# Thirteen low parts from GpSimd to VectorE, and small reorderings, in a one-core decoder step

## The chip, the core and the metric

The kernel runs on one NeuronCore of a Trainium2 chip. Its engines each work through their own instructions in program order: TensorE (PE, with PEld for its weight loads), VectorE (DVE), ScalarE (ACT), GpSimd (POOL) and SyncE (SP), which here issues the DMAs. They meet through semaphores. The metric is the device time of one launch in microseconds (us), as the median of several runs; beside it there is one profiled execution, from which all trace rows come.

## The reference

One layer of a decoder with three parallel branches is computed in float32 for 1024 prompt positions and 32 sample positions (8 sequences of 4), 1056 columns together, with a model width of 1024.

```python
h = _rmsnorm(x, norm_g)
p = h @ w_in                    # ret q, k, v, g | sgu u, v | xattn q | three gates
o_ret = retention(q, k, v, g)   # 4 heads, rotary, chunks of 128, group norm, silu gate
o_sg = _sgu_branch(gelu(su), gelu(sv), sg_ln_g, sg_ws, sg_bs)    # spatial gating unit
o_x = _xattn(xq, mk, mv)        # 4 heads into 256 memory tokens
merged = g_ret * (o_ret @ w_br_ret) + g_sg * (o_sg @ w_br_sg) + g_x * (o_x @ w_br_x)
x = x + merged @ w_o
z = _rmsnorm(x, norm_ffn_g) @ w_up
zc = conv_b + sum(conv_w[j] * zp[:, j:j + L] for j in range(3))  # causal, width 3
a, b = split(zc)
x = x + (gelu(a) * b) @ w_down
y = _rmsnorm(x, norm_final_g)
```

## The kernel before

**Three products for one.** Activations lie with the model dimension on the 128 partitions and the 1056 positions along the free dimension. Every float32 product is made as three products of a reduced type: each operand is split into a high part (a cast, on ACT) and a low part (operand minus high part, a `tensor_tensor` subtraction on DVE or POOL), and PE adds high x high, high x low and low x high in PSUM.

**Weight slabs.** The weights come as slabs of 128 x 1024 in the order of `SLABS`. `w_prep` loads a slab two ahead, casts it on ACT (line 152) and subtracts on POOL (`ptt`, line 117) or, for the slabs listed in `LO_DVE`, on DVE (`vtt`, line 114). At most three slabs are alive in most stages; `w_ahead` prepares the next one at fixed places of a product, usually right after its first eighth (k = 0) and its fourth (k = 3). In the trace a slab's parts are called `wh` and `wl`.

**The order of the work** is written out by hand. Each engine runs its instructions strictly in the order in which the program issues them. `hook()` is called after each eighth of a product (`fm`) or after each row tile (`tm`): it counts down the entries of `later(n, fn)`, which run n hooks on, takes one entry of the `side` list, and adds `rate[0]` to a counter; each time this reaches one, the next step of the first generator in `gens` is issued. So the small work of the neighbouring stage is laid between the large products. Entries of `later` leave their list in order only.

**The stages**, with the names that the change touches:

- *Heads 0 to 3*: q, k, g and v products, with retention of the head before beside them. In head 0, `fm2` interleaves q and k while the input is loaded. `xnorm` beside it sums the squares of x (tile `xr`, DVE additions), splits the sum (`rsh`, `rsl`), multiplies it by ones on PE and forms the reciprocal root `rst`. `rope_evac` evicts q and k: a product with cos on DVE, swapped halves copied by ACT, a product with sin on POOL, and an addition on DVE by `later(4, ...)`.
- *Gating unit*: products su and sv; `ln_row` normalizes rows; `sgu()` multiplies four groups of 128 rows per step (`sgW`), adds a bias (`sgt`, from PSUM) and multiplies into `su`, both on DVE. The products xq 1 to 3 run at the same time, and slabs xq 2 and xq 3 are prepared in the first half of xq 1.
- *Cross-attention*: the generator `xattn(h)` for each head, beside the gate products gb 0 to 7. Its steps are listed in one table (XA scores, XB transposes, XC values, Y for the samples; `KS`, `VS` and `QS` split keys, values and queries). `gate(key)` makes a gate product, evicts it on DVE (`th`) and returns `gate_out`: a tanh on ACT, and three hooks later a store.
- *Output product*: 8 tiles (m) for each of two halves of 528 columns, with one slab per tile and half, `("wo", m, half)`, and two PSUM banks in turn. After each tile DVE adds it to `x2c`, ACT squares, DVE adds to `ssq`. During the second half the generator `half_norm` works on the first: the sums are split (`ns`), PE multiplies them by ones, DVE scales each `x2c` and makes its low part `xl`; two steps per tile. `early1` adds sums of weights for the next stage (`fs`).
- *Up product, convolution, gate*: pairs of slabs by a seven-product scheme, taps of the convolution on DVE (`c`).
- *Down product*: 22 slabs in groups of two (`down(g)`), eight tiles each; DVE adds every tile to `x2t` (`x` in the trace). `last_conv`, the last pair's five convolution steps, runs as a generator beside group 0, one step per hook with `rate[0] = 1.0`.
- *Final norm*: the last two groups run chunk by chunk over the columns (512, 288, 256). `fin_evac` adds tiles, squares (`sq`, ACT) and sums (`ssf`, DVE). `fin(c)` for the first two chunks is a generator: it splits the sums (`sy3`, `sy` in the trace), forms the root `rsy` and multiplies out eight `y` on POOL. For the last chunk the sum over m = 0 to 5 is split into `sy3`, and the squares of m = 6 and 7 go into PE's sum directly (`fin_last`).

## Time and profile before

| | |
|---|---|
| median of 3 runs | 1917.12 us (1916.00 to 1917.32) |
| profiled execution, own time | 1916.06 us |
| its span, first to last instruction | 1913.9 us |
| mean granted TensorE clock | 0.991 |
| busy: PE, DVE, POOL, ACT | 97%, 60%, 48%, 34% |
| data moved by DMA | 204.82 MB, 107 GB/s on average |

A row of the timeline gives start, duration, engine, line, operation, output <- inputs by the program's names, shape and count of merged instructions, and in brackets the engine's idle time just before and who ended it. A row of the waits gives the waiting engine, tile and line, who released it, the total, the number of times and the longest. A row of the stretches gives the length, then busy time and instruction count of PE, PEld, DVE, ACT and POOL, the granted clock, the DMA share and GB/s. PE's busy time comes from modelled ends of pipelined products, so its idle gaps are somewhat rough. A line number is often that of a helper, so tiles tell more.

### The profile page before, as it was taken

What the parts mean: (1) busy time and instruction counts of PE and PEld (TensorE: products, weight loads), DVE (VectorE), ACT (ScalarE), POOL (GpSimd) and SP (SyncE); (2) the same over time, 40 slices, a digit from 0 to 9 for tenths busy, and PEclk for the clock granted to TensorE, in tenths of its full rate; (3) what the DMA queues carried; (4) which work ended last, traced back from release to release, by engine and by line L of the source; (5) the groups of instructions that cost most, each with busy time, mean ns of one, the idle gap of its engine ahead of it and who ended that gap; (6) DMA issues with size and microseconds to landing.
All of it is one profiled execution on the core that took longest, in us unless ns stands there. A gap on an engine that the chain in (4) does not pass through costs nothing.

```text
span 1913.9 us, 32100 instructions
## 1 busy us (share of the span) xinstructions
PE 1854.7 (97%) x13369; PEld 1828.0 (96%) x13369; DVE 1144.7 (60%) x1610; ACT 651.8 (34%) x1016; POOL 921.5 (48%) x583
## 2 busy tenths in 40 slices
PE   8899999999999999999999999899999999999997
PEld 8899999999999998999999999899999999999996
DVE  6554545442464479332352267999999999744447
ACT  6333232421233434323211233544344344321204
POOL 2243434221643421555544533577777777754404
PEclk9999999999999999999999999999999999999998
DMA  5112131324133341426632532022222223732202
GB/s 189 54 45 93 44 105 36 132 66 156 56 135 112 124 181 55 135 90 255 241 124 79 189 140 84 34 90 79 68 90 79 67 90 120 252 133 90 76 1 91
DMA packets 59808, 204.82 MB, mean 107 GB/s; under 512 B 6608, under 2 KB 9840, under 8 KB 59664
## 3 DMA queue, kind: packets, MB, share of 16 engines
q1 hardware_dynamic: 59664, 202.78, 30.8%
q8 instruction: 105, 1.72, 0.4%
q14 instruction: 39, 0.32, 0.1%
HBM read 154.34 MB, written 48.41 MB: 106 GB/s over the span
## 4 chain that ended last, share of the span: by engine, by line
PE 50%; DVE 7%; issue 1%; ACT 1%; POOL 1%; DMA 1%; DVEq 0%; SPq 0%; POOLq 0%; ACTq 0%
PE bp L108 25%; PE mp L108 25%; DVE c L120 1%; DVE xl L114 1%; DVE x2c L120 1%; DVE fs L114 1%; DVE ssf L114 0%; DMA opr<-scr 0%; POOL opl L117 0%; DMA wr<-in_wslab 0%; DVE x L114 0%; ACT xh L1153 0%; DVE hx L114 0%; POOL acl L117 0%; POOL wls L117 0%
## 5 line engine op out<-in xcount | busy, mean ns | idle before, releaser
L117 POOL TENSOR_TENSOR wl<-wr,wh 128x1024 fp32r<-128x1024 f32 x107 | 282.7, 2645 | 438.3 <-ACT wh L152 294.7
L108 PE MATMUL bp<-xh,wh 128*128 128x264 f32 (+1 forms) x1376 | 279.2, 284 | 6.8 <-DVE th L114 2.4
L108 PE MATMUL bp<-xh,wl 128*128 128x264 f32 (+1 forms) x1376 | 280.3, 285 | 1.2 <-POOL wl L117 0.7
L108 PE MATMUL bp<-xl,wh 128*128 128x264 f32 (+1 forms) x1376 | 279.8, 285 | 0.0
L108 PEld LDWEIGHTS bp<-xh,wh 128*128 128x128 f32 x1376 | 215.0, 189 | 8.2 <-issue 3.1
L108 PEld LDWEIGHTS bp<-xh,wl 128*128 128x128 f32 x1376 | 215.0, 189 | 1.8 <-POOL wl L117 1.2
L108 PEld LDWEIGHTS bp<-xl,wh 128*128 128x128 f32 x1376 | 214.5, 189 | 0.0
L108 PE MATMUL mp<-hh,wh 128*128 128x384 f32 (+1 forms) x816 | 190.0, 340 | 4.9 <-ACT hh L111 4.8
L108 PE MATMUL mp<-hl,wh 128*128 128x384 f32 (+1 forms) x816 | 179.6, 327 | 0.3 <-DVE hl L120 0.3
L114 DVE TENSOR_TENSOR x<-x,mp 128x288 f32<-128x288 f32 (+3 forms) x167 | 105.7, 676 | 120.6 <-PE mp L108 120.6
L108 PE MATMUL mp<-hh,wl 128*128 128x384 f32 (+1 forms) x816 | 177.6, 324 | 0.0
L117 POOL TENSOR_TENSOR wl<-fs,wh 128x1024 fp32r<-128x1024 f32 x52 | 146.2, 2814 | 50.9 <-ACT wh L1179 50.4
L108 PEld LDWEIGHTS mp<-hh,wh 128*128 128x128 f32 x816 | 136.0, 191 | 7.8 <-ACT hh L111 5.4
L108 PEld LDWEIGHTS mp<-hl,wh 128*128 128x128 f32 x816 | 136.6, 190 | 1.1 <-DVE hl L120 1.0
L108 PEld LDWEIGHTS mp<-hh,wl 128*128 128x128 f32 x816 | 137.0, 189 | 0.0
L108 PE MATMUL mp<-ach,whs 128*128 128x384 f32 (+3 forms) x524 | 124.3, 326 | 4.0 <-DVE x L114 3.1
L120 DVE SCALAR_TENSOR_TENSOR c<-z,hist,c 128x1024 f32<-128x1024 f32 x88 | 125.0, 1420 | 4.3 <-ACT c L111 4.2
L108 PE MATMUL mp<-ach,wls 128*128 128x384 f32 (+3 forms) x524 | 123.7, 325 | 0.0
L108 PE MATMUL mp<-acl,whs 128*128 128x384 f32 (+3 forms) x524 | 123.4, 325 | 0.0
L152 ACT CAST wh<-wr 128x1024 fp32r<-128x1024 f32 x86 | 89.4, 1043 | 95.8 <-PE mp L108 54.2
L1179 ACT CAST wh<-fs 128x1024 fp32r<-128x1024 f32 x55 | 57.7, 1050 | 155.6 <-DVE fs L114 145.3
L120 DVE SCALAR_TENSOR_TENSOR c<-zs,hist,c 128x32 f32<-128x32 f32 x88 | 110.6, 1256 | 0.0
(367 smaller groups left out, 4161.5 us busy)
## 6 DMA issues: line engine op xcount, KB each, us to landing
wr<-in_wslab SPq DMA_DIRECT2D x162, 512.0 KB, 3.7
sg<-th SPq DMA_DIRECT2D x24, 528.0 KB, 5.2
th<-sg SPq DMA_DIRECT2D x24, 528.0 KB, 5.5
sca<-c SPq DMA_DIRECT2D x22, 528.0 KB, 3.0
opr<-sca SPq DMA_DIRECT2D x22, 528.0 KB, 4.7
opr<-scr SPq DMA_DIRECT2D x16, 528.0 KB, 7.0
scr<-ort SPq DMA_DIRECT2D x8, 528.0 KB, 7.6
hx<-in_xT SPq DMA_DIRECT2D x8, 528.0 KB, 5.9
```

The lines of the kernel that those rows point to most:

```text
L108: nc.tensor.matmul(out=out, lhsT=l, rhs=r, start=start, stop=stop)
L114: nc.vector.tensor_tensor(out=out, in0=a, in1=b, op=op)
L117: nc.gpsimd.tensor_tensor(out=out, in0=a, in1=b, op=op)
L120: nc.vector.scalar_tensor_tensor(out=out, in0=a, scalar=s, in1=b, op0=op0, op1=op1)
L152: nc.scalar.copy(out=hi, in_=raw)
L1179: nc.scalar.copy(out=hi, in_=src)
```

## The change

- `LO_DVE` grows: the low parts of the eight slabs of the output product's second half, of xq 2 and 3, and of the first head's g 0, g 1 and (v, 0, 0) are subtracted on DVE.
- The rotary addition of the first head runs 7 hooks after its eviction, not 4.
- In the table of `xattn`, the next head's query split `QS` moves ahead of its second key split `KS`.
- The tanh of the gb gates, with the store behind it, runs two hooks after the product.
- `last_conv` advances by one step per two hooks.
- In `fin`, the first chunk's first four `y` are multiplied on DVE; the second chunk's norm starts two steps later.
- The last chunk's sum has a tile of its own, `sy4`, and holds m = 0 to 2 only; the five squares of m = 3 to 7 go into PE's sum directly.

```diff
 LO_DVE = [k for i, k in enumerate(SLABS) if k[0] in ("km", "vm") and i % 2] + [("sv", 0, 0), ("sv", 0, 1)]
+LO_DVE += [("wo", m, 1) for m in range(8)]
+LO_DVE += [("xq", 2), ("xq", 3), ("g", 0), ("g", 1), ("v", 0, 0)]
...
-            later(4, lambda: vtt(out, out, sw, ALU.add))
+            later(4 if h else 7, lambda: vtt(out, out, sw, ALU.add))
...
                            (XC, 1), (XB, 2), (XA, 3), (YC, 0), (XC, 2), (KS, h + 1, 0), (XB, 3), (YC, 1),
-                           (KS, h + 1, 1), (XC, 3), (QS, h + 1), (YD,)):
+                           (QS, h + 1), (KS, h + 1, 1), (XC, 3), (YD,)):
...
-            gate(("gb", m))()
+            later(2, gate(("gb", m)))
...
         gens.append(last_conv())
-        rate[0] = 1.0
+        rate[0] = 0.5
...
-        sy3 = slot("sy3", F32R)
+        sy3, sy4 = slot("sy3", F32R), slot("sy4", F32R)
...
-            yield
+            for _ in range(3 if c else 1):
+                yield
...
-                    ptt(y[:, i, 0:w], x2t[m + i][:, c0:c0 + w], r, ALU.mult)
+                    (vtt if c == 0 and m < 4 else ptt)(y[:, i, 0:w], x2t[m + i][:, c0:c0 + w], r, ALU.mult)
...
-            mm(a, ones, sy3[:, 0:w], stop=False)
-            mm(a, ones, sy3[:, w:2 * w], start=False, stop=False)
-            for i in range(2):
-                mm(a, f(ones), sqs[i], start=False, stop=(i == 1))
+            mm(a, ones, sy4[:, 0:w], stop=False)
+            mm(a, ones, sy4[:, w:2 * w], start=False, stop=False)
+            for i in range(len(sqs)):
+                mm(a, f(ones), sqs[i], start=False, stop=(i == len(sqs) - 1))
...
-                if c == 2 and m > 5:
+                if c == 2 and m > 2:
                     last_sq.append(sqs[m])
...
-            if c == 2 and us[-1] == 5:
-                nc.scalar.copy(out=sy3[:, 0:w], in_=ssf[:, sl])
-                vtt(sy3[:, w:2 * w], ssf[:, sl], f(sy3[:, 0:w]), ALU.subtract)
+            if c == 2 and us[-1] == 2:
+                nc.scalar.copy(out=sy4[:, 0:w], in_=ssf[:, sl])
+                vtt(sy4[:, w:2 * w], ssf[:, sl], f(sy4[:, 0:w]), ALU.subtract)
```

## The prediction

> **What bounds the kernel now.** I read the head of the page first.

> ```profile
> span 1913.9 us, 32100 instructions
> PE 1854.7 (97%) x13369; PEld 1828.0 (96%) x13369; DVE 1144.7 (60%) x1610; ACT 651.8 (34%) x1016; POOL 921.5 (48%) x583
> ```

> TensorE (PE) sets the time, and the change takes no product away from it. What can be won is PE's idle time, 1913.9 - 1854.7 = 59 us, and any time that PE works at a lower clock. So I read next who kept PE waiting (us in total, times, longest).

> ```profile
> PE ap L108 <- ACT rsh L337: 5.9, 1, 5.9
> ...
> PE mp L108 <- DVE x L114: 3.1, 2, 2.6
> PE ap L108 <- DVE sgt L114: 3.0, 1, 3.0
> PE mp L108 <- DVE x2c L120: 2.7, 2, 2.0
> ...
> PE ap L108 <- DVE xql L114: 2.1, 1, 2.1
> PE ap L108 <- ACT sy L319: 1.9, 1, 1.9
> PE ap L108 <- DVE ns L114: 1.7, 1, 1.7
> PE ap L108 <- DVE pt L114: 1.6, 3, 0.9
> ...
> PE ap L108 <- ACT xt L111: 1.3, 1, 1.3
> ```

> These nine rows hold 23 us, nearly all behind VectorE (DVE). Each lies in a stage that the change touches: rsh in the first head, sgt in the gating unit, xql, pt and xt in cross-attention, ns and x2c in the output product's second half, x in the down product, sy in the final norm. Then the stretches in which the granted clock (the figure ahead of the DMA share) is about a half:

> ```profile
> 48.70:52.10 3.40, 0.69 (x1) 0.29 (x1) 3.40 (x3) 2.19 (x3) 0.12 (x1) 0.52 0.14 54
> 52.10:55.50 3.40, 3.19 (x11) 3.19 (x12) 0.71 (x2) 1.69 (x2) 3.40 (x9) 0.50 0.06 4
> ...
> 530.00:533.40 3.40, 2.98 (x12) 2.98 (x13) 3.18 (x6) 0.00 (x0) 0.00 (x0) 0.52 0.84 274
> 1154.60:1158.10 3.50, 3.50 (x19) 3.50 (x18) 3.50 (x3) 1.34 (x2) 2.64 (x1) 0.53 0.19 73
> ...
> 1656.40:1659.80 3.40, 2.83 (x10) 2.86 (x11) 3.40 (x5) 1.45 (x2) 3.40 (x2) 0.52 0.20 38
> 1891.90:1895.30 3.40, 3.08 (x14) 3.08 (x15) 3.15 (x7) 1.47 (x4) 2.64 (x2) 0.52 0.41 154
> ```

> Each follows one of the stalls of 1.9 us or more, lasts 3.4 us, and costs a busy PE half of that, 1.7 us. A long stall is thus paid nearly twice. The stall of 2.1 us (xql) has no such stretch, so about 2 us is where it becomes a matter of position.

> **What makes DVE late.** Rows of DVE and GpSimd (POOL) in order of time:

> ```profile
> 43.78 2.38 POOL L117 TENSOR_TENSOR wl<-wr,wh 128x1024 fp32r<-128x1024 f32 x1
> ```

> ```profile
> 44.34 5.52 DVE L114 TENSOR_TENSOR xr<-xr 128x1056 f32<-128x1056 f32 x3 [4.19 <-ACT xr L111]
> 49.77 1.25 DVE L114 TENSOR_TENSOR k<-k,sw 128x1056 f32<-128x1056 f32 x1
> ```

> ```profile
> 728.33 1.23 DVE L114 TENSOR_TENSOR wl<-fs,wh 128x1024 fp32r<-128x1024 f32 x1 [1.17 <-ACT wh L1179]
> ```

> Three additions cost 5.52 us where one of their size costs 1.25: 5.52 - 3.75 = 1.77 us too much, just the time until POOL's subtraction ends (43.78 + 2.38 - 44.34 = 1.82). While POOL subtracts, a DVE instruction with two SBUF operands stands. So a low part moved from POOL to DVE takes a block of up to 2.4 us away and adds 1.23 us of DVE's own.

> **The change part by part**, against the profiled run (1916.06 us with the 2.2 us around its span).

> *First head.* Slab (v,0,0) is the 43.78 row. On DVE its low part falls into the 4.19 us in which DVE waits for ScalarE (ACT), so 1.77 us come back. The two g slabs held earlier additions in the same way, and K's eviction behind them; I count 0.8 more for that, nothing to 1.8 as bounds. The later addition (7 hooks for 4) changes only which of two equal ones (1.25) stands between the sums and the low part rsl: Q's now, K's before. Sum **-2.6**, from -1.0 to -4.3 (one of the two half-clock stretches may go).

> *Gating unit.*

> ```profile
> 523.79 5.98 DVE L114 TENSOR_TENSOR su<-su,sgt 128x512 f32<-128x512 f32 x1
> ```

> ```profile
> 523.30 1.27 POOL L117 TENSOR_TENSOR sgS<-sgS,sgW 32x512 f32<-32x512 f32 x1 [0.71 <-DVE sgS L886]
> 524.54 4.67 POOL L117 TENSOR_TENSOR wl<-wr,wh 128x1024 fp32r<-128x1024 f32 x2
> ```

> One product takes 5.98 us because POOL runs three instructions in a row; the last two are xq 2 and 3, the moved ones. After the change DVE does 2 x 1.23 us ahead of its first sgt, and PE, whose third group needs that one's bank, waits for it: 1.2 us, or 2.4 if sgS (1.27) comes between. The stall of 3.0 becomes 1.2 to 2.4, and the half-clock stretch goes surely at 1.2 and by half a chance at 2.4. **-2.4**, from -0.5 to -3.5.

> *Queries split sooner.*

> ```profile
> 590.79 2.55 DVE L114 TENSOR_TENSOR xql<-xq,xqh 128x1056 fp32r<-128x1056 f32 x1 [3.15 <-ACT xqh L293]
> ```

> The split comes one step earlier, ahead of the key split: it no longer lies behind a slab's cast on ACT nor under that slab's subtraction. The eviction of the gate product queues behind it on DVE for some 1.3 us; its bank is wanted only a whole product later, which covers that (uncovered it would cost these 1.3). The stall of 2.1 goes. **-2.1**, from -1 to -2.1.

> *Tanh later.*

> ```profile
> 643.43 1.18 ACT L111 ACTIVATE th<-th,vecs 128x1056 f32<-128x1056 f32 x1 [0.63 <-DVE xrc L976]
> ```

> ```profile
> 699.07 2.47 DVE L120 SCALAR_TENSOR_TENSOR hx<-hx,vecs,rst 128x1056 f32<-128x1056 f32 x1
> ```

> Behind each tanh on ACT stand the slab's cast, and through it POOL's subtraction, and the cast of pt: 1.18 us sooner for both. That covers the 0.9 of pt; and a subtraction that ends earlier no longer doubles hx, on which xt (1.3) waits. The tanh itself lands two hooks on, perhaps ahead of another softmax; its store moves with it and is read long after. **-1.5**, from -2.9 to +1.

> *Output product, second half.*

> ```profile
> 1087.15 1.05 ACT L152 CAST wh<-wr 128x1024 fp32r<-128x1024 f32 x1 [1.48 <-DMA wr<-in_wslab]
> ```

> ```profile
> 1122.27 2.45 DVE L114 TENSOR_TENSOR ns<-ssq,ns 128x528 fp32r<-128x528 f32 x1 [0.76 <-ACT ns L1476]
> ...
> 1146.37 0.71 DVE L114 TENSOR_TENSOR ssq<-ssq,sq 128x528 f32<-128x528 f32 x1 [0.71 <-ACT sq L111]
> 1146.99 0.69 DVE L114 TENSOR_TENSOR fs<-fr 128x512 f32<-128x512 f32 x1
> 1147.60 2.88 DVE L114 TENSOR_TENSOR fs<-fr,fs 128x512 f32<-128x512 f32 x1
> 1150.40 0.76 DVE L120 SCALAR_TENSOR_TENSOR x2c<-x2c,vecs,rst 128x528 f32<-128x528 f32 x1
> 1151.08 0.70 DVE L114 TENSOR_TENSOR xl<-x2c,xh 128x528 fp32r<-128x528 f32 x1
> ...
> 1167.30 0.71 DVE L120 SCALAR_TENSOR_TENSOR x2c<-mp,x2c 128x528 f32<-128x528 f32 x1 [1.96 <-PE mp L108]
> ...
> 1173.12 0.71 DVE L120 SCALAR_TENSOR_TENSOR x2c<-mp,x2c 128x528 f32<-128x528 f32 x1 [2.59 <-PE mp L108]
> ```

> PE gives a tile each 1173.12 - 1167.30 = 5.82 us. DVE's turn for one, unblocked: eviction 0.71, wait for the square 0.71, sum 0.71, two scalings and two low parts 2 x (0.76 + 0.70) = 2.92; that is 5.05, and with a moved low part 6.3, more where it waits for ACT's cast (1.05, queued behind the square): some 6.7. Two turns add 2 x 0.69 for fs. So for four tiles DVE is slower than PE, with one tile's grace, since there are two banks. Before, POOL added blocks like 2.88 - 0.69 = 2.2 to each turn. Walking through the turns I get 0.6 at the norm (the first low part, 1.23, stands ahead of ns, in place of a block of 2.45 - 0.71 = 1.7), then 1.1 and 1.7 at the banks: 3.4 against 1.7 + 2.7 = 4.4. The longest is below 1.9, so the stretch at 1154.60 goes too (1.7). **-2.7**, from -6.1 (all of it) to +3 (each long turn 1 us longer than I have it). The first two of the eight low parts are made in the first half, where DVE has no scalings and low parts (the 2.92) to do and waits for PE; they cost nothing there, and 1.23 each if DVE were full.

> *Last convolution at half the rate.*

> ```profile
> 1653.17 2.42 DVE L120 SCALAR_TENSOR_TENSOR c<-zs,hist,c 128x32 f32<-128x32 f32 x1
> ```

> A 32-column tap takes 2.42 us under POOL's subtractions, and with one tap after each of five tiles the evictions (x) fall behind: 3.1 us of stall and the stretch at 1656.40, 4.8 in all. With one tap after every second tile DVE has two tiles' time for it. I keep 0.9 for one blocked tap. **-3.9**, from -1.9 to -4.8.

> *Norms at the end.*

> ```profile
> 1883.26 11.28 POOL L117 TENSOR_TENSOR y<-x,rsy 128x512 f32<-128x512 f32 x8 [68.59 <-DVE rsy L120]
> ```

> ```profile
> 1884.10 3.71 DVE L114 TENSOR_TENSOR ssf<-ssf,sq 128x288 f32<-128x288 f32 x3
> ```

> ```profile
> 1903.55 1.13 PE L108 MATMUL ap<-sq,ones 128*128 128x256 f32 x4 [0.44 <-ACT sq L111]
> ```

> POOL's eight y stretch DVE's sums; the sums make sy late (1.9) and bring the stretch at 1891.90 (1.7). Four y go to DVE, two of them ahead of the evictions on which PE's next chunk waits: +0.7 to +2. The second norm starts two hooks on, so sy is ready, but its y's run later and can lie beside the last norm on POOL and DVE: +0 to +2. Three more squares go into the closing sum, which per square costs 1.13 / 2 = 0.57, some 1.7, in place of ACT's and DVE's chain of about the same length. I take **0**, from -3.6 to +2.5.

> **The sum** is -2.6 - 2.4 - 2.1 - 1.5 - 2.7 - 3.9 = -15.2: 1916.06 to 1900.9, and as the median of the runs shown (1917.12) lies 1.06 higher, **1902 us**.

> [...]

> **Rivals.** (1) *DVE inherits.* It takes POOL's place as the late one: the product's turns are 7.5 instead of 6.7, so that its stalls and stretch stay (0), the gating unit gives 0.6, the tail costs 2.5, tanh gives 1.0, the convolution 2.2; with 2.6 and 2.1 that is -6.0: **1911**. For it: turns longer than 5.82. Against: 2.2 us blocks go. (2) *The half-clock stretches stay* wherever they fall, and only stalls shrink: without the clock's share (1.2 in the gating unit, 1.7 each in the product, the convolution and the tail) the sum is -8.9: **1908**. For it: the stall of 2.1 without a stretch. Against: six stretches, each behind a stall. (3) *Slower: the evictions stand behind the slabs.* On POOL nobody stands behind a low part that waits for a cast; on DVE the evictions do. If slabs m2 to m7 come late by the 1.48 us of the row above, a turn is 6.7 + 1.5 = 8.2: six tiles cost 2.4 each, 14.3, and a stretch behind each, 10.2; less the 6.1 of before that is +18.4, against -12.5 elsewhere: **1923**. It decides from about 1.2 us of lateness (then +16.3). Against: in the second half no cast waits so long. (4) *The wait only changes sides*: DVE's own 1.23 and POOL's shifted work eat what the blocks gave, and 2 us remain: **1915**. [...]

> **How the numbers follow.** Forecast 0.55, (1) 0.22, (2) 0.09, (4) 0.08, (3) 0.06. Below 0.2% (3.8 us) this kernel's runs tell no change. Faster is the forecast, (1) and (2): 0.86; same is (4): 0.08; slower is (3): 0.06. All lower bounds together would give 1890; the range goes three quarters of the way there from the forecast, to 1893, and up to 1912, which takes in rivals 1 and 2; the forecast's own is 1896 to 1908.

> **What would show it.** No POOL subtraction beside the additions before rsh, and rsh near 48.3; su without a 6 us row; no xql among PE's waits; DVE turns near 6.7 in the output product, with stalls of 1 to 1.7 and no half clock there; no half clock in the down product. I am wrong if PE waits longer for x2c than 2.7 in total, if the tail after the last product grows by over 2 us, or if stretches at half clock number as many as before.

## The result and the profile after

The changed kernel takes **1900.57 us** (median; 1900.39 to 1901.69), the kernel before 1916.56 us beside it: ratio 0.9918, 95% interval 0.9901 to 0.9935. That is 16.0 us faster, the interval lies well below 1, and it is 1.4 us below the forecast of 1902. The profiled execution went from 1916.06 to 1901.69 us; of the four runs of the changed kernel it is the slowest, by 1.1 us. The sum came out; several of its terms did not.

The head of the page after the change, and the waits of PE in that trace (total, times, longest):

```profile
span 1899.8 us, 32104 instructions
PE 1851.4 (97%) x13375; PEld 1827.2 (96%) x13375; DVE 1141.8 (60%) x1624; ACT 652.1 (34%) x1016; POOL 888.0 (47%) x566
```

```profile
PE mp L110 <- DVE x L116: 6.8, 5, 2.0
...
PE ap L110 <- ACT rsh L339: 3.1, 1, 3.1
...
PE mp L110 <- DVE x2c L122: 1.2, 2, 0.9
...
PE ap L110 <- DVE sgt L116: 0.9, 1, 0.9
...
PE ap L110 <- DVE ns L116: 0.6, 1, 0.6
...
PE ap L110 <- ACT sy L321: 0.2, 1, 0.2
```

Of the nine rows shown for before, xql, pt and xt are gone; sgt fell from 3.0 to 0.9, rsh from 5.9 to 3.1, x2c from 2.7 to 1.2, ns from 1.7 to 0.6, sy from 1.9 to 0.2. One grew: x, from 3.1 to 6.8 (two waits of 2 us in the down product, two new ones of 1.6 and 0.7 in the tail). The stretches at half clock that are left before the closing chain, in the same columns as before:

```profile
47.92:51.33 3.41, 1.87 (x5) 1.47 (x6) 3.41 (x3) 3.38 (x4) 1.50 (x1) 0.50 0.00 0
51.33:54.75 3.42, 3.42 (x13) 3.42 (x12) 2.58 (x2) 0.90 (x2) 3.42 (x11) 0.50 0.37 107
...
1211.87:1215.28 3.41, 3.23 (x14) 3.23 (x15) 3.38 (x5) 2.23 (x5) 1.97 (x3) 0.50 0.47 144
```

There are two more, at 225.4 (as before) and at 1652.2 in the down product. Gone are those of the gating unit, the output product and the tail.

**Where the time went.** PE's instructions are the same in both traces, in the same order up to number 13301. So the start of instruction k after, less its start before, is all that was won up to there, whatever the waits are called:

| PE instruction | start before | start after | shift | in this stage |
|---|---|---|---|---|
| 224, ahead of rsh | 44.84 | 45.50 | +0.66 | start and load +0.66 |
| 1400, head 1 | 220.84 | 219.28 | -1.56 | first head -2.2 |
| 3500 | 517.25 | 515.92 | -1.33 | +0.2 |
| 3590 | 534.67 | 529.86 | -4.80 | gating unit -3.5 |
| 4010 | 596.72 | 589.45 | -7.27 | queries' split -2.5 |
| 4760 | 706.69 | 693.75 | -12.94 | cross-attention, pt and xt -5.7 |
| 7650 | 1117.59 | 1104.29 | -13.30 | -0.4 |
| 7960 | 1161.88 | 1144.54 | -17.34 | output product -4.0 |
| 11700 | 1625.83 | 1609.68 | -16.15 | up product +1.2 |
| 13200 | 1876.09 | 1862.17 | -13.92 | down product +2.2 |
| end of span | 1913.94 | 1899.83 | -14.11 | tail -0.2 |

The +0.66 at the start is within what the load varies between executions: over the kernels below it lies between -0.6 and +0.9. Each kernel has one trace, so a stage's shift holds for one execution.

### The profile page after: what moved, and what is told of

Its sections match the earlier page's. It is cut to its first block, busy times and chain, and to the rows that moved or that the text cites. A ratio compares the mean times of both kernels' runs of the same rounds, so it can differ in the third digit from the quotient of the medians.

```text
span 1899.8 us, 32104 instructions
## 1 busy us (share of the span) xinstructions
PE 1851.4 (97%) x13375; PEld 1827.2 (96%) x13375; DVE 1141.8 (60%) x1624; ACT 652.1 (34%) x1016; POOL 888.0 (47%) x566
## 4 chain that ended last, share of the span: by engine, by line
PE 52%; DVE 7%; issue 1%; ACT 1%; DVEq 0%; POOL 0%; ACTq 0%
PE bp L110 27%; PE mp L110 25%; DVE c L122 2%; DVE xl L116 1%; DVE x2c L122 1%; DVE x L116 0%; DVE fs L116 0%; DVE wl L116 0%; DVE hx L116 0%; DVE z L116 0%; ACT xh L1155 0%; DVE ssf L116 0%; DVE c L116 0%; ACT sq L113 0%; DVE y L116 0%
## 5 line engine op out<-in xcount | busy, mean ns | idle before, releaser
L119 POOL TENSOR_TENSOR wl<-wr,wh 128x1024 fp32r<-128x1024 f32 x94 | 250.5, 2669 | 374.2 <-ACT wh L154 223.2
L122 DVE SCALAR_TENSOR_TENSOR c<-z,hist,c 128x1024 f32<-128x1024 f32 x88 | 129.9, 1477 | 4.6 <-ACT c L113 4.5
```

The lines of the kernel that those rows point to most:

```text
L119: nc.gpsimd.tensor_tensor(out=out, in0=a, in1=b, op=op)
L122: nc.vector.scalar_tensor_tensor(out=out, in0=a, scalar=s, in1=b, op0=op0, op1=op1)
```

## The experiments

All kernels start from the changed one; each was timed beside the kernel before (medians 1916.45 to 1916.69 us), and its ratio is to that. Medians alone don't settle parts of 1 to 3 us here (the runs of one kernel lie up to 6 us apart; more at the end), so each part is read from PE's positions too.

**The last convolution at full rate again.**

```diff
-        rate[0] = 0.5
+        rate[0] = 1.0
```

> The changed kernel with the last convolution at its full rate again (one step after each tile, as before). In the changed kernel's trace PE waits 1.96 and 2.04 us for x in the down product and has a half-clock stretch at 1652.2; the same products of PE lie 2.1 us later than the shift ahead of the stage would put them. Theory A (the steps were only moved to where POOL subtracts without a pause; at the full rate two of the four taps come before the first subtraction, 1.5 us each in place of up to 5.8): the stage gives 2 us back, about 1898.5 us. Rival B (the stalls come from the phase in which slabs reach POOL, whatever the rate): within 0.5 us of the changed kernel, 1900 to 1901. Rival C (the forecast's reading, half the rate wins): 1903 or more.

1899.85 us, ratio 0.9912 (0.9897 to 0.9926). From instruction 11700 to 13200 PE loses 0.3 us against before, where the changed kernel loses 2.2. PE waits 0.5 and 2.6 us for x and has one stretch. The median gained only 0.7. Rival C, the forecast's reading, is out, for it asked for 1903 or more. Theory A would have it that half the rate costs the 1.9 between the two traces, and that is not shown: the six kernels below that keep half the rate lie between -0.7 and +0.7 us against before in this stage, so much of the changed kernel's 2.2 goes with the moment at which POOL's slabs arrive, as rival B has it (in its trace a subtraction lies on the second small tap too, 2.46 us where the six others have 0.24). Which of the two rates is better stays open. What the traces do show is that the taps become dearer at half the rate. DVE in the changed kernel (start, duration):

```profile
1630.06 1.28 DVE L122 SCALAR_TENSOR_TENSOR c<-z,hist,c 128x1024 f32<-128x1024 f32 x1
1631.26 2.46 DVE L122 SCALAR_TENSOR_TENSOR c<-zs,hist,c 128x32 f32<-128x32 f32 x1
1633.65 2.53 DVE L116 TENSOR_TENSOR x<-x,mp 128x768 f32<-128x768 f32 x4
1636.11 3.24 DVE L122 SCALAR_TENSOR_TENSOR c<-z,hist,c 128x1024 f32<-128x1024 f32 x1
1639.27 2.44 DVE L122 SCALAR_TENSOR_TENSOR c<-zs,hist,c 128x32 f32<-128x32 f32 x1
1641.63 2.54 DVE L116 TENSOR_TENSOR x<-x,mp 128x768 f32<-128x768 f32 x4
```

A tap is two instructions, over 1024 and over 32 columns. The third, at 1636, costs 3.24 + 2.44 = 5.7 us, two tiles of PE (2.9 each), and so does the fourth. In the other six traces at half rate they cost 4.6 to 5.2 and 5.8, at the full rate 3.8 and 4.6. Behind each the evictions come two at a time (x4), and PE has waited. POOL beside them has no gap:

```profile
1635.86 2.41 POOL L119 TENSOR_TENSOR wls<-wr,whs 128x1024 fp32r<-128x1024 f32 x1 [2.18 <-ACT whs L154]
1638.21 3.44 POOL L119 TENSOR_TENSOR acl<-opr,ach 128x1056 fp32r<-128x1056 f32 x1
1641.61 4.73 POOL L119 TENSOR_TENSOR wls<-wr,whs 128x1024 fp32r<-128x1024 f32 x2
```

**The last convolution at twice the rate.**

```diff
-        rate[0] = 0.5
+        rate[0] = 2.0
```

> The changed kernel with the last convolution at twice the full rate: two steps after each tile, so that all four taps lie in the first two tiles' turns. Theory A (what counts is to be done before POOL's first low part of the stage, about 7 us after the first eviction): taps cost 1.3 to 1.9 + 0.24 us each, a turn of DVE is 1.4 + 3.2 = 4.6 us against 2.9 us of a tile on PE, twice, so one stall of about 1.5 to 2 us in place of 4.0 and the stretch: 2 to 4 us faster than the changed kernel, 1897 to 1898.5. Rival B (evictions behind two taps each are as late as behind one that is blocked): stalls of 2 us and a stretch stay, 1900 to 1901.

1903.86 us, ratio 0.9933 (0.9916 to 0.9949): slower than the changed kernel, which neither theory had. DVE in this kernel:

```profile
1628.86 1.28 DVE L122 SCALAR_TENSOR_TENSOR c<-z,hist,c 128x1024 f32<-128x1024 f32 x1
1630.06 2.41 DVE L122 SCALAR_TENSOR_TENSOR c<-zs,hist,c 128x32 f32<-128x32 f32 x1
1632.39 3.47 DVE L122 SCALAR_TENSOR_TENSOR c<-z,hist,c 128x1024 f32<-128x1024 f32 x1
1635.79 2.33 DVE L122 SCALAR_TENSOR_TENSOR c<-zs,hist,c 128x32 f32<-128x32 f32 x1
1638.04 1.31 DVE L116 TENSOR_TENSOR x<-x,mp 128x768 f32<-128x768 f32 x2
```

POOL's subtractions began at 1629.85, too soon for the third tap's small half and for the fourth tap. The two taps took 9.2 us between one eviction and the next (1628.86 to 1638.04), and PE waited 7.2 us. That POOL is what makes a tap dear stands; that all four would be through before it starts was wrong, and two blocked taps in a row are worse than two apart.

**Tanh at once again.**

```diff
-            later(2, gate(("gb", m)))
+            gate(("gb", m))()
```

> The changed kernel with the tanh of the gate product issued at once again, not two hooks later. Between PE's positions 594 and 706 us of before the changed kernel gained 5.4 us, where the forecast had 1.5. Theory A (the tanh did it: ahead of the casts of slab and pt it delays both by its 1.18 us, at three or more tiles): nearly all of it is lost, 4 to 5.5 us, 1904.5 to 1906. Rival B (tanh gives the 1.5 of the forecast, and the rest comes from the queries' split and the low parts moved to DVE): 1902. Rival C (it does nothing by itself): within 0.5 us of the changed kernel.

1904.80 us, ratio 0.9939 (0.9924 to 0.9954). The stage of pt and xt gives back 5.7 us, all that it had gained, and its waits return: 0.29, 0.86 and 0.36 us for pt, 1.30 for xt. Theory A.

**The eight low parts of the output product back on POOL.**

```diff
-LO_DVE += [("wo", m, 1) for m in range(8)]
```

> The changed kernel with the eight low parts of the output product's second half back on POOL. The stage (PE's positions 1124 to 1160 of before, and the 0.3 ahead of it) gained 4.0 us in the changed kernel, where the forecast had 2.7. Theory A (it is all by these low parts): 4 us are lost, 1904.5. Rival B (part of it is the phase in which DVE and POOL reach the stage, 13 us sooner by the other parts): 1 to 3 lost, 1901.5 to 1903.5. Rival C (they only change sides): within 0.5 us of the changed kernel.

1902.45 us, ratio 0.9927 (0.9912 to 0.9942). The waits of before return, 1.7 for ns and 0.7 and 2.0 for x2c, and the stage gives back 2.9 of its 4.0. What it doesn't give back, 1.2, is about the price of the stretch at half clock that stood behind the 2.0 before and does not here. The profiled run wins nearly all of this back in the down product (2.6), where the changed kernel's stretch and its wait of 0.5 are missing; the median is 1.9 above the changed kernel's. Rival B by the number, for a reason that it did not name.

**Three parts undone in three stages.**

```diff
-LO_DVE += [("xq", 2), ("xq", 3), ("g", 0), ("g", 1), ("v", 0, 0)]
+LO_DVE += [("xq", 2), ("xq", 3)]
...
-                           (QS, h + 1), (KS, h + 1, 1), (XC, 3), (YD,)):
+                           (KS, h + 1, 1), (XC, 3), (QS, h + 1), (YD,)):
...
-            for _ in range(3 if c else 1):
-                yield
+            yield
...
-                    (vtt if c == 0 and m < 4 else ptt)(y[:, i, 0:w], x2t[m + i][:, c0:c0 + w], r, ALU.mult)
+                    ptt(y[:, i, 0:w], x2t[m + i][:, c0:c0 + w], r, ALU.mult)
...
-                if c == 2 and m > 2:
+                if c == 2 and m > 5:
...
-            if c == 2 and us[-1] == 2:
+            if c == 2 and us[-1] == 5:
```

> The changed kernel with three parts undone that lie in different stages, so that PE's positions tell them apart: slab (v,0,0) and the two g slabs back on POOL (first head), the queries' split back in its old place (cross-attention), the norms at the end as before. In the changed kernel the same products of PE moved by -2.3 in the first head, -2.5 at the queries' split and -0.2 from the last convolution to the end. Theory A (each gain belongs to its own part): the positions go back by 1.5 to 3 (the clock's stretches there move), 2.5, and 0.2, in all about 1905.5 us. Rival B (the queries' stall was removed by the low parts xq 2 and 3 on DVE, not by the split's place): nothing is lost at the split, 1903. Rival C (the new norms lose what PE gains, and the old ones are better now): the tail gives 1 us back or more.

1900.60 us (1899.11 to 1905.06), ratio 0.9922 (0.9907 to 0.9937), no slower than the changed kernel. Against it the positions go back by 2.4 in the first head, as expected, by **0.03** at the queries' split, and the tail is 1.2 us *shorter*. Two more differences, -0.7 in the up product and -2.5 in the down product, belong to no part undone: the first has no cause that I know, and in the second a wait of 2.0 is 0.5. So the low parts of g and v are worth their 2.4. For the split rival B has the number (the wait did not come back); the cause that it names, the low parts of xq 2 and 3, falls further below, where the split and the tanh are both undone. For the tail rival C holds in this trace, where no stretch follows a wait of 2.0 for sy.

**The later addition and xq 2 and 3 undone.**

```diff
-            later(4 if h else 7, lambda: vtt(out, out, sw, ALU.add))
+            later(4, lambda: vtt(out, out, sw, ALU.add))
...
-LO_DVE += [("xq", 2), ("xq", 3), ("g", 0), ("g", 1), ("v", 0, 0)]
+LO_DVE += [("g", 0), ("g", 1), ("v", 0, 0)]
```

> The changed kernel with two parts undone in different stages: the later addition of the first head back at 4 hooks, and slabs xq 2 and 3 back on POOL. Theory A (the gating unit's 3.5 us belong to these two low parts; the later addition does nothing, as the forecast had it): PE's positions go back by 3.5 us between 517 and 535 us of before, by nothing at rsh: 1904. Rival B (the addition holds the sums of the first head, and the low part of v only makes room): 1 us or more is lost at rsh too, 1905. Rival C (low parts on DVE do not matter in the gating unit: the stall shrank because all comes 1.5 us sooner): below 1 us lost, 1901.

1905.86 us, ratio 0.9944 (0.9929 to 0.9959). The gating unit gives back 3.6 us, with its wait of 3.0 and its stretch: theory A there. At rsh 1.2 us are lost, the wait grows from 3.1 to 4.2: rival B there. DVE in this kernel, and then in the changed one:

```profile
40.93 2.53 DVE L116 TENSOR_TENSOR wl<-wr,wh 128x1024 fp32r<-128x1024 f32 x1 [3.38 <-ACT wh L154]
43.38 1.25 DVE L116 TENSOR_TENSOR q<-q,sw 128x1056 f32<-128x1056 f32 x1
44.55 3.83 DVE L116 TENSOR_TENSOR xr<-xr 128x1056 f32<-128x1056 f32 x3
```

```profile
41.42 2.52 DVE L116 TENSOR_TENSOR wl<-wr,wh 128x1024 fp32r<-128x1024 f32 x1 [3.39 <-ACT wh L154]
43.87 3.83 DVE L116 TENSOR_TENSOR xr<-xr 128x1056 f32<-128x1056 f32 x3
47.62 1.25 DVE L116 TENSOR_TENSOR q<-q,sw 128x1056 f32<-128x1056 f32 x1
```

The low part waits for ACT's cast, and Q's addition then stands behind it and ahead of the three sums. The later addition takes it out of there. (The three sums are 3.83, their 3 x 1.25, in place of 5.52.)

**The 32-column taps off DVE**, for the last convolution's four taps, at its full rate.

```diff
+            def tap_off(self, j):
...
+                t = small("tc", [P, 8, 4], 1)
+                act(t, self.zs[:, :, j:j + 4], scale=self.w(j))
+                ptt(self.cs, self.cs, t, ALU.add)
...
-            pa.tap(1)
+            pa.tap_off(1)
...
-        rate[0] = 0.5
+        rate[0] = 1.0
```

The other three calls of `tap` change in the same way.

> The changed kernel with the last convolution at full rate, and its four 32-column taps taken off DVE: ACT scales the columns into a small tile and POOL adds them. Beside the kernel with the full rate alone (1899.85 us; stalls of 0.53 and 2.58 us for x, and a half-clock stretch at 1642). Theory A (what makes the evictions late is that each blocked tap costs DVE a whole POOL subtraction, whatever its size: two 32-column taps of 2.4 us): the first stall goes, the second shrinks by its 2.4 us and takes the stretch of 1.7 with it: 3 to 4.8 us less, 1895 to 1897. Rival B (the blocked 1024-column taps and the sum, 2.2 us and more each, are enough to make the evictions late): stalls of 1.5 us or more stay, 1898 to 1899.5. Rival C (POOL's added work makes the low parts late): 1900 or more.

1897.97 us, ratio 0.9903 (0.9888 to 0.9917). The first wait goes; a wait of 2.0 and its stretch stay; the stage is 1.5 us shorter than at full rate alone. Between A and B: the small taps were part of it. What is left is the closing product of the convolution, beside two of POOL's subtractions, with two tiles' evictions behind it:

```profile
1638.53 3.51 DVE L116 TENSOR_TENSOR c<-c 128x1056 f32<-128x1056 f32 x1 [1.51 <-POOL c L119]
1641.97 2.53 DVE L116 TENSOR_TENSOR x<-x,mp 128x768 f32<-128x768 f32 x4
```

**Another tail.**

```diff
-            for _ in range(3 if c else 1):
+            for _ in range(2 if c else 1):
...
-                    (vtt if c == 0 and m < 4 else ptt)(
+                    (vtt if c == 0 and m > 3 else ptt)(
```

> The changed kernel with the last four y of the first norm on DVE in place of the first four, and the second norm two hooks on in place of three. In the changed kernel PE waits 1.59 and 0.66 us for x in the tail, behind the y on DVE, and the last chain of DVE and ACT takes 2.8 us more than before, 1.65 of it beside POOL's y of the second norm. Theory A (both come from where the y are): the 1.6 goes, and 0.5 to 1 of the end: 1898 to 1899. Rival B (the stalls move to a later eviction, and the second norm's sums are again too late for PE): within 0.5 us of 1900.6, with PE waiting for sy. Rival C: the wait for sy comes back with its stretch, 1902.

1900.37 us, ratio 0.9919 (0.9902 to 0.9935). Of the waits for x the 0.7 goes and 1.5 stays, now behind y 4 and 5; a wait of 2.1 for sy comes back, with a stretch at 1880.3. From instruction 13200 to the end that is +0.5, the stretch included, for -0.2. Rivals B and C.

**Queries' split and tanh both undone.**

```diff
-                           (QS, h + 1), (KS, h + 1, 1), (XC, 3), (YD,)):
+                           (KS, h + 1, 1), (XC, 3), (QS, h + 1), (YD,)):
...
-            later(2, gate(("gb", m)))
+            gate(("gb", m))()
```

> The changed kernel with the queries' split back in its old place and the tanh issued at once again, both. With the split alone undone the wait for xql did not come back, nor with the tanh alone undone. Theory A (either of the two takes the wait away, so neither undone alone brings it back): with both undone PE waits about 2.1 us for xql again and its positions between 590 and 597 us go back by 2.5, beside the 5.7 of the tanh at later products; 1907. Rival B (the wait went with the low parts moved to DVE or with the 3 us by which everything comes sooner): no wait for xql, 1904.8 as with the tanh alone undone.

1908.08 us, ratio 0.9953 (0.9937 to 0.9969). The wait is back:

```profile
587.05 0.39 PE L110 MATMUL ap<-mmh,xql 128*128 128x256 f32 x1 [2.09 <-DVE xql L116]
```

A stretch follows it at 588.6, which before did not have, and between instructions 3590 and 4010 the kernel loses 3.9 us against the changed one. Theory A: either edit takes the wait away alone, and the low parts of xq 2 and 3, on DVE here too, do not. With the split late but the tanh later (the kernel with three parts undone) ACT shows how:

```profile
583.84 1.05 ACT L154 CAST wh<-wr 128x1024 fp32r<-128x1024 f32 x1
584.79 1.06 ACT L295 CAST xqh<-xq 128x1056 fp32r<-128x1056 f32 x1
585.76 1.18 ACT L113 ACTIVATE th<-th,vecs 128x1056 f32<-128x1056 f32 x1
```

The tanh now follows the queries' cast; with both undone it stood ahead of it and of the slab's cast.

**The closing product on POOL too.** On top of the kernel without 32-column taps on DVE:

```diff
-            conv_end(NFF - 1, pa, pb)
+            conv_end(NFF - 1, pa, pb, ptt)
...
-        def conv_end(j, a, b):
-            vtt(b.c, b.c, a.c, ALU.mult)
+        def conv_end(j, a, b, sub=vtt):
+            sub(b.c, b.c, a.c, ALU.mult)
```

> The kernel whose four 32-column taps went to ACT and POOL (1897.97 us), and with the closing product of the last convolution on POOL too. There DVE ran this product for 3.51 us beside POOL's subtractions, an eviction stood behind it, PE waited 2.01 us for x, and a half-clock stretch followed. Theory A (DVE's long blocked instructions between evictions are what is left of the stage's wait): the 2.0 goes and the stretch of 1.7, 1894 to 1896. Rival B (POOL is full in this stage, so its 2.5 us more make the low parts late): PE waits for wls or acl instead, 1897 or more.

**1895.21 us**, ratio 0.9887 (0.9873 to 0.9902). PE no longer waits for x in the stage. DVE waits for PE between evictions instead, and POOL takes the product:

```profile
1641.73 1.32 DVE L116 TENSOR_TENSOR x<-x,mp 128x768 f32<-128x768 f32 x2 [1.57 <-PE mp L110]
```

```profile
1641.16 2.50 POOL L119 TENSOR_TENSOR c<-c 128x1056 f32<-128x1056 f32 x1
```

Theory A. The stage is 5.0 us shorter than before, and 7.2 shorter than in the changed kernel's trace (4.3 to 5.7 shorter than in the six others at half rate). The next two kernels, which share it, show the same 5.0.

**Two other tails on that kernel.** First, only the last two y of the first norm on DVE:

```diff
-                    (vtt if c == 0 and m < 4 else ptt)(
+                    (vtt if c == 0 and m > 5 else ptt)(
```

> As the kernel with the closing product on POOL, and of the first norm only the last two y on DVE, in place of the first four. Theory A (the waits of 1.59 and 0.66 us for x in the tail are those of evictions behind y on DVE; the last two y have no eviction that PE waits for behind them): 1 to 2 us less than that kernel. Rival B (six y on POOL hold DVE's sums of squares, as before the change, and the second norm's sums come late): within 0.5 us of it, or more.

1895.75 us, ratio 0.9890 (0.9875 to 0.9905). The waits for x are gone, and PE waits 3.1 us for sy instead, with two stretches: rival B.

Second, the whole tail of before, the last four edits of the kernel with three parts undone:

```diff
-            for _ in range(3 if c else 1):
-                yield
+            yield
...
-                if c == 2 and m > 2:
+                if c == 2 and m > 5:
```

> As the kernel with the closing product on POOL, and the whole tail as before the change (all y of the first two norms on POOL, second norm one hook on, two squares in the closing sum). With three parts undone the positions from the last convolution to the end went back by -1.2 us, that is, the old tail was shorter, where no half-clock stretch fell into it. Theory A (the old tail is 1.2 us shorter but for its stretch of 1.7): 1.2 less than that kernel, or 0.5 more where the stretch falls. Rival B (the new tail is better, as PE's waits for sy are gone): 1 us or more longer.

1894.78 us, ratio 0.9885 (0.9868 to 0.9901). From instruction 13200 to the end the old tail costs exactly what it did before (0.0), the new one -0.2, the one with the last two y on DVE +1.2. The medians cannot tell the three tails apart; in the traces they differ by where PE waits and whether a stretch falls there.

These three kernels are 4.8 to 5.8 us below the changed one by their medians. The intervals of the ratios just touch the changed kernel's; the profiled spans, 1893.9, 1893.6 and 1894.1 us beside 1899.8, and the stage itself, -5.0 in all three beside -0.7 to +2.2 in the seven at half rate, say the same.

## Why the prediction was right, and where it was wrong

| term | forecast | measured |
|---|---|---|
| first head | -2.6 | -2.2 (-1.6 to -3.0 in the kernels that share it) |
| gating unit | -2.4 | -3.5 |
| queries split sooner | -2.1 | -2.5, but not by this edit alone |
| tanh later | -1.5 | -5.7 |
| output product | -2.7 | -4.0 |
| last convolution | -3.9 | **+2.2** (-0.7 to +0.7 in the six others at this rate) |
| norms at the end | 0 | -0.2 |
| not foreseen | | +1.7 (start +0.7, up product +1.2, rest -0.2) |
| sum | -15.2 | -14.1 |

The total is right because one term, 6 us off and of the wrong sign in this trace, was offset by four whose gains were sized too small, by 7.0 together. That is luck: nothing ties the one to the others. The forecast's case, DVE late by POOL's blocks and relieved by taking low parts over, holds in the three stages where the parts were moved. Rivals 1 and 4 fell with the output product and the gating unit, rival 3 with DVE's turns there, rival 2 with the missing stretches. Two readings in the forecast were loose without bearing on the sum: of the 23 us of waits "nearly all behind" DVE, 9.1 stand behind ACT (rsh, sy and xt), whose cast for rsh in turn waits for DVE's additions; and at 1.2 us of lateness rival 3 gives +16.6, not +16.3.

*Last convolution.* The step that failed: "with one tap after every second tile DVE has two tiles' time for it", at 0.9 for one blocked tap. It priced the 32-column half only (2.42) and did not ask what POOL does where the later taps now fall. They meet a POOL without gaps, where the large half is blocked too: 5.7 us, two whole tiles. So the wider spacing gave about what the dearer taps took: in the seven traces at half rate the term lies between -0.7 and +2.2, nowhere near -3.9. Whether the full rate is better is not shown (+0.3 in its one trace); what helps is to take the instructions off DVE (-5.0 in three traces).

*Tanh.* Mechanism right (casts 1.18 us sooner), size wrong. The forecast summed waits of 0.9 for pt and part of xt's 1.3. The stretch from instruction 4010 to 4760, before and after:

```profile
596.72:706.69 109.97, 106.51 (x751) 102.28 (x751) 62.17 (x115) 45.19 (x94) 44.13 (x22) 1.00 0.45 153
```

```profile
589.45:693.75 104.30, 104.30 (x751) 102.63 (x751) 57.02 (x117) 45.59 (x96) 43.45 (x22) 1.00 0.50 169
```

PE's idle time, 109.97 - 106.51 = 3.46, went to nothing, and 2.2 more came out of its *busy* time, at the same 751 instructions and the same clock. A product is shown 0.28 us long though the next starts 0.12 later; so a wait also shows as a product that overlaps with nothing. At the waits shown as 0.28, 0.93, 0.36 and 1.32 the positions jump by 0.55, 1.20, 0.62 and 1.57: each cost 0.25 to 0.3 more than its row says. The other 1.7 of the 5.7 lie at places where the trace before shows PE idle for 0.2 us or less.

*Queries' split.* The wait went as forecast. That the earlier split did it was the step that fell: undone alone it brings nothing back, and neither does the tanh. The forecast had listed each under its own term; one wait can't be won twice, and with either edit alone it would have gone.

*Gating unit.* DVE and POOL in the changed kernel:

```profile
521.75 2.34 DVE L116 TENSOR_TENSOR wl<-wr,wh 128x1024 fp32r<-128x1024 f32 x2
524.02 0.67 DVE L116 TENSOR_TENSOR sgt<-ap,sgC 128x512 f32<-128x512 f32 x1
524.73 1.05 DVE L116 TENSOR_TENSOR su<-su,sgt 128x512 f32<-128x512 f32 x1
```

```profile
521.97 3.25 POOL L119 TENSOR_TENSOR sgS<-sgS,sgW 32x512 f32<-32x512 f32 x1 [0.71 <-DVE sgS L888]
```

The two low parts stand ahead of the first sgt as foreseen, and su has no row of 6 us. The wait is 0.9 and not 1.2 to 2.4, because sgS waited for DVE (3.25 for 1.27) instead of coming between; the stretch went.

*First head.* Right within what the clock leaves open. Its step "the later addition changes only which of two equal ones stands between the sums and rsl" was wrong: without it 1.2 of the gain is lost. rsh starts at 47.73; the forecast had it near 48.3. Both windows at half clock stayed.

*Output product.* Turns were shorter than the 6.7 of the forecast. From one eviction of x2c to the next on DVE:

```profile
1130.20 0.69 DVE L122 SCALAR_TENSOR_TENSOR x2c<-mp,x2c 128x528 f32<-128x528 f32 x1
...
1137.16 0.70 DVE L122 SCALAR_TENSOR_TENSOR x2c<-mp,x2c 128x528 f32<-128x528 f32 x1
...
1139.52 1.23 DVE L116 TENSOR_TENSOR wl<-wr,wh 128x1024 fp32r<-128x1024 f32 x1 [0.24 <-ACT wh L154]
...
1142.76 0.70 DVE L122 SCALAR_TENSOR_TENSOR x2c<-mp,x2c 128x528 f32<-128x528 f32 x1
```

The first, with the two fs, is 7.0, the second 5.6, already below PE's 5.82: it holds one scaling and not two, and waits 0.24 for ACT's cast, where I had allowed 0.4. So the waits are 0.3 and 0.9, not 1.1 and 1.7.

*Norms at the end.* DVE in the changed kernel's tail, and POOL at its end:

```profile
1869.20 2.39 DVE L116 TENSOR_TENSOR y<-x,rsy 128x512 f32<-128x512 f32 x2
1871.52 1.17 DVE L116 TENSOR_TENSOR x<-x,mp 128x288 f32<-128x288 f32 x3
```

```profile
1886.43 8.32 POOL L119 TENSOR_TENSOR y<-x,rsy 128x288 f32<-128x288 f32 x10 [10.76 <-DVE rsy L122]
```

Gains and losses of the size of the bounds met. The wait for sy and its stretch are gone (-3.5, a new wait of 0.7 included), a wait of 1.6 for evictions behind y on DVE came (+1.8), and from instruction 13330 to the end 1.5 are lost: the closing sum takes 1.2 more with five squares for two, and DVE's last chain 1.65 more beside POOL's y of the second norm (its first three steps on the reciprocal root 0.72, 0.90 and 0.90 us each, where they took 0.41 to 0.43), less the 1.3 that PE no longer waits just ahead of the sum. After the last product of the down product the time to the end grew by 0.6, and after PE's very last instruction by 1.7; neither is the 2 that would have spoken against me.

Of the signs named ahead, rsh, su, xql and the output product without half clock came as told; half clock in the down product did not go. The stretches fell from eight to five, the closing one among them.

*Up product.* +1.2 us over 390, spread evenly: 3203 instructions with 390.29 us of busy time for 389.22, and no wait in it. From instruction 8600 on, where the changed kernel loses 1.1, nine of the twelve kernels above lose 0.8 to 1.1, the other three 0.0, 0.5 and 2.0. I have no cause for it.

## What to carry to other kernels

Measure a change by when the same instruction starts, not by the waits that the profile names: a wait costs more than its row (by 0.25 to 0.3 us at four waits here), and two edits can be paid by the same one. Take more than one trace of a stage before a difference of 2 us is called the edit's: the same code gave -0.7 to +2.2 here. Before small work is spread out in time, look at what the other engine does in the time that it is moved *to*; where each instruction that overlaps pays a whole one of the other engine (here 2.33 to 2.48 us for a tap of 0.24), taking them away helped (the stage 5.0 us shorter than before with five of them off DVE) and small size did not. An engine with evictions that others wait for is best relieved of the work that nobody waits for.

## What the runs showed of the hardware

```profile
591.58:594.99 3.41, 1.59 (x11) 1.59 (x12) 3.23 (x5) 0.09 (x1) 0.65 (x1) 1.00 0.48 76
594.99:598.41 3.42, 3.42 (x26) 3.38 (x26) 0.78 (x3) 0.93 (x4) 0.00 (x0) 1.00 1.01 400
1151.37:1154.78 3.41, 1.44 (x13) 1.25 (x12) 2.70 (x5) 2.14 (x4) 0.00 (x0) 1.00 0.43 158
1154.78:1158.20 3.42, 3.42 (x18) 3.42 (x17) 3.42 (x3) 1.16 (x2) 2.64 (x1) 0.50 0.14 54
```

The wait of 2.1 for xql began ahead of a boundary: 1.82 us of the window are idle, and the next is at full clock (1.00). The wait of 2.0 for x2c fell into one window, 1.97 idle, and the next is at half (0.50). With the low parts back on POOL the same wait of 1.97 is cut in two by a boundary, and nothing follows:

```profile
1136.55:1139.97 3.42, 1.92 (x16) 1.70 (x14) 3.42 (x6) 1.26 (x2) 0.00 (x0) 1.00 0.52 153
1139.97:1143.38 3.41, 2.94 (x24) 2.97 (x25) 2.70 (x4) 2.23 (x3) 1.39 (x1) 1.00 0.20 79
```

Over all traces of this study, between 40 us and the tail and leaving out windows that were at half themselves (many are the same stall in another kernel), 52 of 52 windows with 1.9 us or more idle are followed by half clock, 3 of 5 with 1.80 to 1.90, and none of 67 with 1.0 to 1.8; in the traces before and after alone it is 10 of 10, none of 1 and none of 7. So 1.9 us of 3.41, some 55% of a window, was enough each time, and a stall of about 2 us has a stretch in one run and none in another, 1.7 us each time: the wait for xql is 2.1 before, and nothing follows; with the split and the tanh undone it is 2.09, 1.86 us of its window (585.20 to 588.61) are idle, and the next is at 0.50. That this is also what sets the runs of one kernel with a few such stalls as far apart as 1899.11 and 1905.06 us (three parts undone) is not shown; the granted clock was 0.995 in the one and 0.990 in the other.

**DVE beside POOL's subtractions.** A 32-column tap of the last convolution took 0.24 us alone and 2.33 to 2.48 beside POOL's subtractions, nearly what POOL's whole instruction took (2.4). Evictions, with one input from PSUM, took the same beside them and alone, a tile's two 1.30 to 1.32. POOL's own next one (acl), where it overlapped a tap's 1024 columns or the closing product by some 1.1 us, took 3.42 to 3.52, against 2.48 at the median of all 21. It went the other way too: sgS on POOL took 3.25 us in place of 1.27 under two of DVE's low parts.
